# The MLP of a hybrid Mamba-2/S5 block as one row of 112 steps, with six low parts formed by transfer

## The chip, the cores and the metric

The kernel runs on one core of a Trainium2 chip. The metric is the device time of one execution in microseconds; the kernel before is given with three runs and their median. A profile is one execution recorded by the hardware profiler. PE is TensorE, DVE VectorE, ACT ScalarE, POOL GpSimd, SP SyncE.

## The reference

One decoder block over 512 tokens of width 1024, with 16 meta tokens ahead of them, all in float32. Two mixers (a Mamba-2 SSD and an S5) run side by side on one input projection and feed one output projection; then comes an MLP with a squared ReLU, and a last norm:

```python
        mix = jnp.concatenate([y_ssd.astype(h.dtype), y_s5.astype(h.dtype)], axis=-1)
        h = h + mix @ w_out[layer]
        m = _rmsnorm(h, g_mlp[layer]) @ w_up[layer]
        h = h + jnp.square(jax.nn.relu(m)) @ w_down[layer]
    return _rmsnorm(h, g_final)[:, N_META:].astype(x.dtype)
```

`w_up` is 1024 x 4096 and `w_down` 4096 x 1024. The change concerns the MLP alone, the last 350 us of some 820.

## The kernel before

**Numbers in two parts.** TensorE multiplies a shortened float32 (`F32R`). To keep the precision, each operand is split into a high part (ACT rounds it: `A.copy(hi, src)`) and a low part (DVE subtracts: `lo = src - hi`), and each product is three matmuls: high by high, high by low, low by high. The helper is `split_into` (L992 on); `split_w` makes `whi` and `wlo` of a weight block of 128x1024 numbers, `split_a` makes `ah` and `al` of an activation block of 128x512. Each of these four names has three buffers. Another way to a low part is used earlier in the kernel (L121, L122): ACT writes `-hi` into `lo`, and a DMA issued by POOL adds the source to it in memory. `add_to` (L990) is such an adding DMA.

**Fewer products.** The MLP's two matrix products are done blockwise with Strassen's scheme in the form of Winograd: 7 block products for 8, for which sums of weight blocks and of activation blocks are formed first. The hidden width is done in four quarters, each in two groups g = 0 and 1 of 512 columns.

- *Up stage* of a quarter: 14 steps, seven products (P1 to P7) for each group. A step is 24 matmuls of 256 columns with a block of `w_up` as weights and one of the token operands `opA`, `opB`, `opC` (differences of the normed tokens, `TOK`). The weights of P5, P6 and P3 are sums in a buffer of the tile `quad`: s1 = block 10 + block 11 (DVE, `vadd`), s2 = s1 + block 00 (DVE), and block 01 added by DMA for P3. P7's is block 10 plus block 00 by DMA. The products end in the tile `r`, with the squared ReLU on ACT, and additions by DVE after P2, P7 and P3.
- *Down stage* of a quarter: 14 steps, seven products for each group, named by their activations: 11, S1, S2, 12, S3, S4, 22 (`PRODUCTS`). A step is 12 matmuls of 512 columns. S1 to S4 are differences of blocks of `r` made by DVE; the weights are blocks of `w_down` or their sums T1 (DVE), T2, T3 and T4 (DMA). After a product's second group DVE adds its two banks in PSUM to the running hidden state `h_tok` (L876).

**What sets the order.** The program is written quarter by quarter: `up_blocks`, then `block_product`. Weight loads, sums and splits stand in regions of high priority (`AHEAD`), and a scheduler decides where they go on each engine; loads start as soon as a buffer is free (`quad` has six, `raw` three). Each engine executes its instructions in its own order, and an instruction that waits holds up all behind it on that engine. SP issues the loads, POOL the adding DMAs, each in order.

**Start of the MLP.** The tokens' tiles 0 and 1 give `opA`. Tiles 2 and 3 (`late`) are normed into `xs`, transposed by PE into `pt` (`turned`, L939), and combined into `opB` and `opC`. In the first quarter P1 and P2 of group 0 and P1 of group 1, which need `opA` alone, come first.

Of the kernel before, what the change touches and what calls it, by code (L numbers as in the profile page):

```python
# [53 lines left out]
def hybrid_block_kernel(ctx, tc, x, meta_tokens, g_mix, w_in, conv_w, conv_b, dt_bias, a_log, d_ssd,  # L54
# [8 lines left out]
    def dump(name, ap):  # L63
        if name in dbg:
# [6 lines left out]
    ps = ctx.enter_context(tc.tile_pool(name="ps", bufs=8, space=PSUM))  # L71
# [4 lines left out]
            "pq2": "q", "pdt": "q", "pa": "q", "par": "q", "u0": "mm"}  # L76
# [861 lines left out]
    def turned(t, k):  # L938
        pt = bank("pt")  # L939
# [41 lines left out]

    def sub(out, a, b):
        V.tensor_tensor(out=out, in0=a, in1=b, op=ALU.subtract)  # L983
# [8 lines left out]
    def split_into(hi, lo, src, by_dma=False):  # L992
        A.copy(hi, src)  # L993
        sub(lo, src, hi.bitcast(F32))
# [7 lines left out]
    def split_a(src):  # L1002
        hi = ml.tile(list(src.shape), F32R, tag="ah", name="ah", bufs=3)
        lo = ml.tile(list(src.shape), F32R, tag="al", name="al", bufs=3)
        split_into(hi, lo, src)
        return hi, lo

    def quad():
        return ml.tile([P, 2, 512], F32, tag="quad", name="quad", bufs=6)

    def up_room(raw=False):
        t = wp.tile([P, KD, P], F32, tag="raw", name="raw", bufs=3) if raw else quad()
        return t.rearrange("p a b -> p (a b)").rearrange("p (k c) -> p k c", k=4)


    t2 = up_room()
    opB = slot("opB", [P, 2, 2, 4, HT], F32R)
    opC = ml.tile([P, 3, 2, 4, HT], F32R, tag="opC", name="opC", bufs=1)
    for t in late:
        c = slice((t - 2) * P, (t - 1) * P)  # L1020
        for k in range(2):
            src = turned(t, k)
            if k == 0:
                sub(H[:, 0, 0, :, c], src, H[:, 0, 0, :, c])
                t1 = H[:, 0, 0, :, c]
            else:
                sub(t2[:, :, c], src, t1)
            A.copy(H[:, k, 1, :, c], src)
        for o, src in ((0, t2[:, :, c]), (1, t1)):
            split_into(opB[:, o, 0, :, c], opB[:, o, 1, :, c], src)  # L1030
    h12, h21, h22 = H[:, 0, 1], H[:, 1, 0], H[:, 1, 1]
    sub(h12, h12, h22)
    split_into(opC[:, 0, 0], opC[:, 0, 1], h12)
    A.mul(opC[:, 1, 0], h22, -1.0)
    neg_sub(opC[:, 1, 1], h22, opC[:, 1, 0].bitcast(F32))
    sub(t2, h21, t2)
    split_into(opC[:, 2, 0], opC[:, 2, 1], t2)
    TOK = {"P1": opA[:, 0], "P2": opA[:, 1], "P6": opB[:, 0], "P5": opB[:, 1], "P7": opC[:, 0], "P3": opC[:, 1],
           "P4": opC[:, 2]}

    class Cols:
# [7 lines left out]
        def load(self, i, k, room):  # L1049
            c0 = (8 * self.q + 4 * self.g + 2 * i) * P  # L1050
            dma(out=room, in_=w_up[0, 512 * k:512 * k + 512, c0:c0 + 2 * P].rearrange("(k p) c -> p k c", p=P))
            self.b[i, k] = room

        def sums(self):
            b = self.b
            if "S1" not in b:
                self.load(1, 0, up_room())
                self.load(1, 1, up_room(True))
                if (0, 1) not in b:
                    self.load(0, 1, up_room(True))  # L1060
                b["S1"] = up_room()
                vadd(b["S1"], b[1, 0], b[1, 1])
                b["S2"] = up_room()
                vadd(b["S2"], b["S1"], b[0, 0])
                add_to(b[1, 0], b[0, 0])

        def get(self, m):
            b = self.b
            if m == "P1":
                self.load(0, 0, up_room(not (self.q == 0 and self.g == 1)))  # L1070
                return b[0, 0]
            if m == "P2":
                if (0, 1) not in b:
                    self.load(0, 1, up_room(True))
                return b[0, 1]
            self.sums()
            if m == "P3":
                add_to(b["S2"], b[0, 1])
            return b[{"P5": "S1", "P6": "S2", "P7": (1, 0), "P3": "S2", "P4": (1, 1)}[m]]

    UP_BANK = {"P1": "X", "P2": "Y", "P5": "Z", "P6": "X", "P7": "X", "P3": "Z", "P4": "X"}
    UP_ORDER = [(g, m) for g in range(2) for m in ("P1", "P5", "P6", "P2", "P7", "P3", "P4")]

    UP_FIRST = [(0, "P1"), (0, "P2"), (1, "P1")] + [(0, m) for m in ("P6", "P5", "P7", "P3", "P4")] + UP_ORDER[8:]

    def up_blocks(q, rs):
        cs = [Cols(q, g) for g in range(2)]
        banks = {}
        for g, m in UP_FIRST if q == 0 else UP_ORDER:
            with tc.high_priority(offset=AHEAD):  # L1090
                w = split_w(cs[g].get(m))
            bk = g, UP_BANK[m]
            first = bk not in banks
            if first:
                banks[bk] = bank(f"u{g}")
            pb = banks[bk].rearrange("p (m t) -> p m t", m=2)
            x = TOK[m]
            n = 0
            for mm in range(2):
                for k in range(4):  # L1100
                    for a, b in ((0, 0), (0, 1), (1, 0)):

                        T.matmul(pb[:, mm], lhsT=w[a][:, k, mm * P:(mm + 1) * P], rhs=x[:, b, k],  # L1103
                                 start=(first and n == 0), stop=(n in (11, 23)), skip_group_check=not (first and mm == 0))
                        n += 1
            r = {(i, t): rs[g][:, i, :, t * HT:(t + 1) * HT] for i in range(2) for t in range(2)}
            if m == "P1":
                A.copy(r[0, 0], pb)
            elif m == "P2":
                sub(r[0, 0], pb, r[0, 0])  # L1110
                relu2(r[0, 0], r[0, 0])
            elif m == "P5":
                A.copy(r[1, 1], pb)
            elif m == "P6":
                A.copy(r[0, 1], pb)
            elif m == "P7":
                vadd(r[1, 1], pb, r[1, 1])
                relu2(r[1, 1], r[1, 1])
            elif m == "P3":
                vadd(r[0, 1], pb, r[0, 1])  # L1120
                relu2(r[0, 1], r[0, 1], -1.0)
            else:
                relu2(r[1, 0], pb)
# [5 lines left out]
    class Rows:  # L1129
# [8 lines left out]
        def load(self, k, n, t):  # L1138
            r0 = (8 * self.q + 4 * self.g) * P
            dma(out=t, in_=w_down[0, r0:r0 + 4 * P, 512 * n:512 * n + 512].rearrange("(j k p) c -> k p j c", k=2, p=P)[k])  # L1140
            self.b[k, n] = t

    def down_blocks(rows):

        t1 = [None, None]
        t1[0], b12a = quad(), quad()
        t1[1], b11b = quad(), quad()
        b11a, b12b = quad(), quad()
        for g, r in enumerate(rows):
            r.load(0, 0, (b11a, b11b)[g])  # L1150
        for g, r in enumerate(rows):
            r.load(0, 1, (b12a, b12b)[g])
            r.load(1, 1, spare_quads[2 + g])
            vadd(t1[g], r.b[0, 0], r.b[0, 1])
            r.b["T1"] = t1[g]
            add_to(r.b[0, 1], r.b[1, 1])
        for g, r in enumerate(rows):
            r.load(1, 0, spare_quads[g])

    def weights_of(r, m):  # L1160
        b = r.b
        if m == "T2":
            add_to(b[0, 0], b[0, 1])
        elif m == "T4":
            add_to(b[0, 0], b[1, 0])
        return b[{"11": (0, 0), "T1": "T1", "T2": (0, 0), "21": (1, 0), "T3": (0, 1), "22": (1, 1), "T4": (0, 0)}[m]]
# [31 lines left out]
    quads = slot("quads", [P, 4, 2, 512])  # L1198
    spare_quads = [quads[:, i] for i in range(4)]

    def block_product(q, rs, done):
        rows = [Rows(q, g) for g in range(2)]
        sums = [Sums(rs[g]) for g in range(2)]
        banks = {}
        with tc.high_priority(offset=AHEAD):
            down_blocks(rows)
        for n, (am, bm, bk) in enumerate(PRODUCTS):
            with tc.high_priority(offset=AHEAD):
                bs = [split_w(weights_of(rows[g], bm)) for g in range(2)]
            as_ = [split_a(sums[g].get(am)) for g in range(2)]  # L1210
            first = bk not in banks
            if first:
                banks[bk] = [bank("acct" if bk == "Y" else "acc") for _ in range(2)]
            order = [(g, s) for g in range(2) for s in range(2)]
            if n == 6:
                order.sort(key=lambda x: x[1])
            if n == 6 and q == 3:
# [112 lines left out]
```

## Time and profile before

| | us |
|---|---|
| three runs | 822.14, 826.29, 823.89; median 823.89 |
| the profiled execution | 820.66 |
| its span in the trace | 819.0 |
| PE busy, matmuls | 773.4 (94%), 4943 |
| DVE busy | 622.6 (76%) |
| ACT busy | 497.9 (61%) |
| POOL busy | 83.3 (10%) |
| MLP, up stage of quarter 0 | 470.5 to 522.2 |
| its down stage | to 561.6 |
| quarters 1, 2 and 3 | to 643.7, 726.8 and the end |

The span is the time from the first to the last recorded instruction. A row of a group of instructions has line, engine, operation, out<-in with the number of them, then the busy time, the mean of one in ns, and the idle time of its engine just before them with what ended it. In the view of waits a row has the waiting engine and line, what it waited for, the sum in us, how often, and the longest. In the timeline a row has start and length in us; in brackets stands how long the engine was idle before and who released it. In the chain of waits a row has start, length and what the time was spent on. A matmul's length holds its way through the array, so matmuls that follow each other closely overlap; their pace is the distance of their starts.

### The profile page before, as it was taken

The page shows a single profiled execution, that of the slowest core. Times are in us where ns is not written, and L with a number is a line of the kernel's source. Part 1 is how long each engine was busy: PE and PEld are TensorE (multiplying, and loading weights), DVE is VectorE, ACT ScalarE, POOL GpSimd, SP SyncE. Part 2 cuts the span into 40 slices and gives each one's busy share as a digit, 9 for nine tenths or more (in the row PEclk, how much of TensorE's full clock was granted, in tenths as well). Part 3 has the DMA queues.
Part 4 walks back from the last instruction along what each step waited for, and adds up shares of the span by engine and source line. Part 5 has one row for each costly group of instructions (what it writes and reads, how often), then busy time and mean ns, then how long its engine had stood idle before and what let it go on. Part 6 is the DMA issues. An engine that isn't in the chain of part 4 may idle for free.

```text
span 819.0 us, 13036 instructions
## 1 busy us (share of the span) xinstructions
PE 773.4 (94%) x4943; PEld 681.4 (83%) x4943; DVE 622.6 (76%) x1002; ACT 497.9 (61%) x806; POOL 83.3 (10%) x133
## 2 busy tenths in 40 slices
PE   6999999899999999999999979899989998999996
PEld 6999898898787778778888879778987898789985
DVE  4489898988785679779435486797769875987797
ACT  7578789988554753546124466654665465546665
POOL 3211000011000110010100010110111011101101
PEclk9999999999999999999999999999999999999998
DMA  8998666767664756356324058873867486747622
GB/s 242 196 226 198 140 162 143 167 146 176 151 152 132 165 133 131 101 126 231 103 99 159 1 138 273 179 181 105 226 157 168 117 216 157 167 123 186 130 51 104
DMA packets 130790, 126.10 MB, mean 154 GB/s; under 512 B 21964, under 2 KB 105848, under 8 KB 130728
## 3 DMA queue, kind: packets, MB, share of 16 engines
q1 hardware_dynamic: 121224, 90.66, 38.7%
q0 software_dynamic: 9504, 34.61, 23.2%
q8 instruction: 39, 0.64, 0.3%
q14 instruction: 23, 0.19, 0.1%
HBM read 83.76 MB, written 6.88 MB: 111 GB/s over the span
## 4 chain that ended last, share of the span: by engine, by line
PE 27%; DMA 15%; issue 14%; DVE 6%; ACT 5%; POOL 2%; SPq 0%; POOLq 0%; ACTq 0%; DVEq 0%
PE acc L832 8%; DMA quad<-raw 6%; PE pv L138 3%; PE pg L138 3%; DMA ab<-aD 3%; PE acc L1233 3%; PE acct L832 3%; DMA quad<-in_w_down_dram 2%; PE u L1103 2%; DVE wlo L983 2%; DMA raw<-in_w_up_dram 2%; ACT whi L993 2%; DVE quad L98 2%; POOL quad L990 1%; PE pyd L776 1%
## 5 line engine op out<-in xcount | busy, mean ns | idle before, releaser
L993 ACT CAST whi<-quad 128x1024 fp32r<-128x1024 f32 x73 | 76.2, 1047 | 68.1 <-PE acc L1233 28.7
L983 DVE TENSOR_TENSOR wlo<-quad,whi 128x1024 fp32r<-128x1024 f32 x73 | 89.0, 1222 | 27.3 <-ACT whi L993 27.3
L1103 PE MATMUL u<-opC,whi 128*128 128x256 f32 x384 | 71.2, 287 | 9.3 <-DVE r L98 4.8
L1233 PE MATMUL acc<-whi,al 128*128 128x512 f32 x184 | 72.5, 394 | 2.6 <-DVE al L983 2.6
L1233 PE MATMUL acc<-wlo,ah 128*128 128x512 f32 x184 | 70.9, 390 | 0.0
L1103 PEld LDWEIGHTS u<-opC,whi 128*128 128x128 f32 x384 | 59.3, 191 | 12.3 <-ACT whi L993 4.2
L1233 PE MATMUL acc<-whi,ah 128*128 128x512 f32 x184 | 65.5, 389 | 0.0
L116 ACT CAST whi<-raw 128x1024 fp32r<-128x1024 f32 x31 | 32.3, 1043 | 50.1 <-PE acc L832 31.5
L117 DVE TENSOR_TENSOR wlo<-raw,whi 128x1024 fp32r<-128x1024 f32 x31 | 38.2, 1232 | 29.6 <-ACT whi L116 29.2
L138 PE MATMUL pxb<-xhi,whi 128*128 128x264 f32 x192 | 55.5, 289 | 1.6 <-ACT xcr L694 1.6
L138 PE MATMUL pxb<-xhi,wlo 128*128 128x264 f32 x192 | 56.1, 292 | 0.0
L138 PE MATMUL pxb<-xlo,whi 128*128 128x264 f32 x192 | 55.8, 291 | 0.0
L1103 PE MATMUL u<-opC,wlo 128*128 128x256 f32 x192 | 53.1, 283 | 0.2 <-DVE wlo L983 0.2
L1103 PE MATMUL u<-opB,whi 128*128 128x256 f32 x256 | 48.2, 287 | 3.1 <-ACT whi L993 3.1
L1103 PE MATMUL u<-opA,whi 128*128 128x256 f32 x256 | 46.4, 280 | 0.0
L1233 PEld LDWEIGHTS acc<-whi,al 128*128 128x128 f32 x184 | 34.6, 188 | 12.0 <-DVE al L983 5.2
L1103 PEld LDWEIGHTS u<-opB,whi 128*128 128x128 f32 x256 | 40.9, 194 | 3.5 <-ACT whi L993 3.3
L121 POOL DMA_DIRECT2D wlo<-raw x26 | 22.3, 856 | 180.2 <-ACT xcr L694 63.4
L1233 PEld LDWEIGHTS acc<-whi,ah 128*128 128x128 f32 x184 | 34.6, 188 | 7.1
L1233 PEld LDWEIGHTS acc<-wlo,ah 128*128 128x128 f32 x184 | 34.6, 188 | 6.8
L1103 PEld LDWEIGHTS u<-opA,whi 128*128 128x128 f32 x256 | 39.5, 188 | 0.3
L122 ACT CAST whi<-raw 128x1024 fp32r<-128x1024 f32 x26 | 27.1, 1043 | 18.7 <-PE pz L138 7.3
(428 smaller groups left out, 2355.3 us busy)
## 6 DMA issues: line engine op xcount, KB each, us to landing
raw<-in_w_in_dram SPq DMA_DIRECT2D x28, 512.0 KB, 4.1
wlo<-raw POOLq DMA_DIRECT2D x26, 512.0 KB, 5.1
raw<-in_w_up_dram SPq DMA_DIRECT2D x23, 512.0 KB, 3.8
raw<-in_w_glu_dram SPq DMA_DIRECT2D x16, 512.0 KB, 4.1
raw<-in_w_out_dram SPq DMA_DIRECT2D x16, 512.0 KB, 3.5
quad<-in_w_down_dram SPq DMA_DIRECT2D x16, 512.0 KB, 5.7
quads<-in_w_down_dram SPq DMA_DIRECT2D x16, 512.0 KB, 4.6
quad<-quads POOLq DMA_DIRECT2D x16, 512.0 KB, 5.3
```

The lines of the kernel that those rows point to most:

```text
L98: V.tensor_tensor(out=out, in0=in0, in1=in1, op=ALU.add)
L116: A.copy(hi, raw)
L117: V.tensor_tensor(out=lo, in0=raw, in1=hi.bitcast(F32), op=ALU.subtract)
L121: G.dma_start(out=lo.bitcast(F32), in_=raw, accum_op=ALU.add)
L122: A.copy(hi, raw)
L138: T.matmul(ps_out, lhsT=w[a][:, k, 0:m], rhs=x[b][:, k, tok], start=(n == 0), stop=(n == len(steps) - 1))
L776: T.matmul(pyd[64 * q:64 * q + 64, o], lhsT=xdt[:, hd], rhs=Gm[h][:, hd % 8])
L832: T.matmul(acc[t], lhsT=lhs[2 * sl + k][a][:, t * P:(t + 1) * P], rhs=wt[b][:, k], start=(sl == 0 and k == 0 and n == 0), stop=(sl == n_sl ...
L983: V.tensor_tensor(out=out, in0=a, in1=b, op=ALU.subtract)
L993: A.copy(hi, src)
L1103: T.matmul(pb[:, mm], lhsT=w[a][:, k, mm * P:(mm + 1) * P], rhs=x[:, b, k], start=(first and n == 0), stop=(n in (11, 23)), skip_group_che ...
L1233: T.matmul(banks[bk][s], lhsT=as_[g][x][:, j, s * P:(s + 1) * P], rhs=bs[g][y][:, j], start=(first and g == 0 and j == 0 and i == 0), stop ...
```

## The change

The MLP is written as one row of 112 steps, 28 for a quarter (14 up, 14 down), numbered from 0. For each step a table (`at`) lists the loads and sums that are issued ahead of it; the split of step i + 2 is issued ahead of step i. Outside of the six places before step 0 no high priority is used. So in this numbering quarter 1 has its up steps at 28 to 41 and its down steps at 42 to 55: 42 and 43 are product 11 of groups 0 and 1, 44 and 45 are S1, 46 and 47 S2, 48 and 49 product 12, then S3, S4, and 54 and 55 product 22.

- Three of the seven activation blocks of each group and quarter (11, 12 and 22, blocks of `r` themselves) get `al` by transfer: ACT's multiplication by -1, then POOL's adding DMA of 128x2x256 numbers. These are 24 in all; DVE subtracts the other 32.
- Product 12 keeps its two banks in PSUM (`ybank`) over all four quarters and is added to `h_tok` once, in the last quarter: six additions fewer.
- PSUM has a pool of its own for the MLP: six banks in turn and the two that stay.
- Buffers: `quad` two instead of six, and a new tile `bquad` with four.
- In the first quarter P5 comes ahead of P6 and the steps of group 1 are mixed among those of group 0, and `opC` is made ahead of step 4.

The core of the diff:

```diff
     def split_into(hi, lo, src, by_dma=False):
-        A.copy(hi, src)
-        sub(lo, src, hi.bitcast(F32))
+        if by_dma:
+
+            A.mul(lo, src, -1.0)
+            add_to(lo.bitcast(F32), src)
+            A.copy(hi, src)
+        else:
+            A.copy(hi, src)
+            sub(lo, src, hi.bitcast(F32))
...
+    class Quarter:
...
+            for g, c in enumerate(self.cols):
+                u = 7 * g
+                self.add(u - 6, c.load(0, 0, raw_room))
+                self.add(u - 4, c.load(1, 0, lambda: as_up(quad())))
+                self.add(u - 2, c.load(1, 1, raw_room))
+                self.add(u - 1, c.s1, c.load(0, 1, raw_room))
+                self.add(u, c.s2)
+                self.add(u + 1, c.s4)
+            for g, c in enumerate(self.rows):
+                d = 14 + g
+                self.add(d - 8, c.load(0, 0, bquad))
+                self.add(d - 6, c.load(0, 1, bquad))
+                self.add(d - 5, c.load(1, 1, lambda g=g: spare_quads[2 + g]))
+                self.add(d - 3, c.load(1, 0, lambda g=g: spare_quads[g]))
+                self.add(d - 3, c.t1)
+                self.add(d - 1, c.t2)
+                self.add(d + 3, c.t4)
...
+        def split(self, i):
+            if i < 14:
+                g, m = self.ups[i]
+                self.w[i] = split_w(self.cols[g].get(m))
+            else:
...
+                n, g = divmod(i - 14, 2)
+                am, bm, _ = PRODUCTS[n]
+                self.w[i] = split_w(self.rows[g].get(bm))
+                self.a[i] = split_a(self.sums[g].get(am), am[0] != "S")
...
+        def done(self, n, s):
+            if n == 3 and self.q < 3:
+                return
...
+    for i in range(112):
+        if i == 4:
+            rest_of_tokens()
+            quads = slot("quads", [P, 4, 2, 512])
+            spare_quads = [quads[:, j] for j in range(4)]
+        ahead(i)
+        split(i + 2)
...
+        quarters[i // 28].run(i % 28)
```

`c.s1` adds blocks 10 and 11 on DVE into a `quad` and issues the DMA that makes P7's weights; `c.s2` adds block 00 on DVE, `c.s4` block 01 by DMA. `t1` adds on DVE and issues the DMA for T3; `t2` and `t4` are DMAs.

The scheduler still moves instructions of this row. The orders below show what stands where. On PE, at the start of the MLP: before, ahead of the first tokens' difference, there are the last product of the output projection (`acct`), two matmuls of the first up steps (`u_4873` is P1 of group 0, `u_4905` P2) and the transposes of tile 2.

```order
L832 MATMUL acct<-sparel,yhi 128x512
L1103 MATMUL u_4873<-opA,whi 128x256
L1103 MATMUL u_4905<-opA,whi 128x256
L941 MATMUL pt<-ident,xs 128x128 x8
L1103 MATMUL u_4873<-opA,whi 128x256
L1103 MATMUL u_4873<-opA,wlo 128x256
```

And the same place of the changed kernel:

```order
L833 MATMUL acct<-sparel,yhi 128x512
L942 MATMUL pt<-ident,xs 128x128 x16
L1220 MATMUL u<-opA,whi 128x256 x2
L1220 MATMUL u<-opA,wlo 128x256
L1220 MATMUL u<-opA,whi 128x256 x2
```

The transposes of tile 3, which stood behind two whole steps, now stand ahead of the first one.

On DVE, in the first steps of the down stage of quarter 1, before (`S_6183` and `S_6189` are S1 of groups 0 and 1; `quad<-quad,raw` is s1 of the next quarter; `al<-r` is the low part of product 11):

```order
L983 TENSOR_TENSOR al<-r,ah 128x512
L983 TENSOR_TENSOR al<-S_6183,ah 128x512
L983 TENSOR_TENSOR wlo<-quad,whi 128x1024
L983 TENSOR_TENSOR S_6189<-r 128x512
L983 TENSOR_TENSOR S_6323<-r 128x512
L986 SCALAR_TENSOR_TENSOR S_6239<-S_6189,r 128x512
L983 TENSOR_TENSOR wlo<-quad,whi 128x1024
L876 TENSOR_TENSOR h_tok<-h_tok,acc 128x512
L983 TENSOR_TENSOR al<-S_6189,ah 128x512
L876 TENSOR_TENSOR h_tok<-h_tok,acc 128x512
L98 TENSOR_TENSOR quad<-quad,raw 128x1024
L983 TENSOR_TENSOR wlo<-quad,whi 128x1024
```

And after (`S_6159` is S1 of group 0, for step 44; `S_6183` S1 of group 1, for step 45; `wlo<-bquad` is T2 of group 0, for step 46):

```order
L993 TENSOR_TENSOR al<-S_6159,ah 128x512
L993 TENSOR_TENSOR wlo<-quad,whi 128x1024 x2
L993 TENSOR_TENSOR S_6183<-r 128x512
L993 TENSOR_TENSOR S_6301<-r 128x512
L996 SCALAR_TENSOR_TENSOR S_6232<-S_6183,r 128x512
L99 TENSOR_TENSOR quad<-quad,raw 128x1024
L993 TENSOR_TENSOR wlo<-bquad,whi 128x1024
L877 TENSOR_TENSOR h_tok<-h_tok,acc 128x512
L993 TENSOR_TENSOR al<-S_6183,ah 128x512
L993 TENSOR_TENSOR al<-S_6207,ah 128x512
L877 TENSOR_TENSOR h_tok<-h_tok,acc 128x512
```

The low part of product 11 is gone from DVE, and s1 of the next quarter now stands ahead of the low part of S1 of group 1, with the split of T2 and an addition to `h_tok` between them.

On POOL, through the same down stage, before (`quad<-quad` is T2):

```order
L990 DMA quad<-quads 128x1024
L990 DMA quad<-quad 128x1024 x2
L990 DMA quad<-raw 128x1024
L990 DMA quad<-quads 128x1024 x2
L990 DMA quad<-raw 128x1024 x2
```

And after (`bquad<-bquad` is T2, `quad<-raw` the addition of s1, `bquad<-quads` T4 of both groups; the first `al` is that of step 43, the four behind are those of steps 48, 49, 54 and 55):

```order
L1000 DMA bquad<-bquad 128x1024 x2
L1000 DMA al<-r 128x2x256
L1000 DMA quad<-raw 128x1024
L1000 DMA bquad<-quads 128x1024 x2
L1000 DMA al<-r 128x2x256 x4
L1000 DMA quad<-raw 128x1024 x2
```

The additions keep their sequence, and the low parts stand among them: one behind T2, four behind T4.

More of the change, by code (lines that the diff above doesn't have):

```diff
@@ L1000, in split_w, with split_a, as_up, raw_room @@
         return hi, lo
-    def split_a(src):
+    def split_a(src, by_dma):
         hi = ml.tile(list(src.shape), F32R, tag="ah", name="ah", bufs=3)
         lo = ml.tile(list(src.shape), F32R, tag="al", name="al", bufs=3)
-        split_into(hi, lo, src)
+        split_into(hi, lo, src, by_dma)
         return hi, lo
+    def as_up(t):
+        return t.rearrange("p a b -> p (a b)").rearrange("p (k c) -> p k c", k=4)
+    def raw_room():
+        return as_up(wp.tile([P, KD, P], F32, tag="raw", name="raw", bufs=3))
     def quad():
[L1009 to L1039, printed above, removed]
+        return ml.tile([P, 2, 512], F32, tag="quad", name="quad", bufs=2)
+    def bquad():
+        return ml.tile([P, 2, 512], F32, tag="bquad", name="bquad", bufs=4)
     class Cols:
@@ L1081, in hybrid_block_kernel @@
-    UP_BANK = {"P1": "X", "P2": "Y", "P5": "Z", "P6": "X", "P7": "X", "P3": "Z", "P4": "X"}
[L1082 to L1123, printed above, removed]
@@ new lines, in f, with s1, s2 @@
+            def f():
+                c0 = (8 * self.q + 4 * self.g + 2 * i) * P
+                self.b[i, k] = t = room()
+                dma(out=t, in_=w_up[0, 512 * k:512 * k + 512, c0:c0 + 2 * P].rearrange("(k p) c -> p k c", p=P))
+            return f
+        def s1(self):
+            b = self.b
+            b["S"] = as_up(quad())
+            vadd(b["S"], b[1, 0], b[1, 1])
+            add_to(b[1, 0], b[0, 0])
+        def s2(self):
+            vadd(self.b["S"], self.b["S"], self.b[0, 0])
@@ L1291, in norm_half_second, with ahead, split, rest_of_tokens @@
                                op1=ALU.mult)
-    for q in range(4):
-        rs = [ml.tile([P, 2, 2, SEQ], F32, tag="r", name="r") for _ in range(2)]
-        up_blocks(q, rs)
-        if q == 3:
+    quarters = [Quarter(q) for q in range(4)]
+    def ahead(i):
+        for qu in quarters:
+            qu.ahead(i - 28 * qu.q)
+    def split(i):
+        if i < 112:
+            quarters[i // 28].split(i % 28)
+    with tc.high_priority(offset=AHEAD):
+        for i in range(-6, 0):
+            ahead(i)
+        split(0)
+        split(1)
+    t2 = as_up(bquad())
+    opB = slot("opB", [P, 2, 2, 4, HT], F32R)
+    opC = ml.tile([P, 3, 2, 4, HT], F32R, tag="opC", name="opC", bufs=1)
+    TOK = {"P1": opA[:, 0], "P2": opA[:, 1], "P6": opB[:, 0], "P5": opB[:, 1], "P7": opC[:, 0], "P3": opC[:, 1],
+           "P4": opC[:, 2]}
+    for t in late:
+        c = slice((t - 2) * P, (t - 1) * P)
+        for k in range(2):
+            src = turned(t, k)
+            if k == 0:
+                t1 = H[:, 0, 0, :, c]
+                sub(t1, src, t1)
+                split_into(opB[:, 1, 0, :, c], opB[:, 1, 1, :, c], t1)
+            else:
+                sub(t2[:, :, c], src, t1)
+                split_into(opB[:, 0, 0, :, c], opB[:, 0, 1, :, c], t2[:, :, c])
+            A.copy(H[:, k, 1, :, c], src)
+    h12, h21, h22 = H[:, 0, 1], H[:, 1, 0], H[:, 1, 1]
+    def rest_of_tokens():
+        sub(h12, h12, h22)
+        split_into(opC[:, 0, 0], opC[:, 0, 1], h12)
+        A.mul(opC[:, 1, 0], h22, -1.0)
+        neg_sub(opC[:, 1, 1], h22, opC[:, 1, 0].bitcast(F32))
+        sub(t2, h21, t2)
+        split_into(opC[:, 2, 0], opC[:, 2, 1], t2)
+    for i in range(112):
[3 more added lines that the diff above has]
+            spare_quads = [quads[:, j] for j in range(4)]
+        ahead(i)
+        split(i + 2)
+        if i == 98:
             os = slot("os", [P, 4, DM])
             sqj = ml.tile([P, SEQ], F32, tag="rl", name="sqj", bufs=1)
-        block_product(q, rs, finish if q == 3 else lambda n, t, ch: None)
+        quarters[i // 28].run(i % 28)
 _INS = ['x', 'meta_tokens', 'g_mix', 'w_in', 'conv_w', 'conv_b', 'dt_bias', 'a_log', 'd_ssd', 'g_ssd', 'lam_re',
```

232 lines of the change are left out of this document (139 added, 93 removed).

## The prediction

> **What bounds the kernel now.** The first part of the page asks which engine is full.
>
> ```profile
> PE 773.4 (94%) x4943; PEld 681.4 (83%) x4943; DVE 622.6 (76%) x1002; ACT 497.9 (61%) x806; POOL 83.3 (10%) x133
> ```
>
> PE is, and the change leaves its 4943 matmuls as they are, so time can only come out of PE's idle stretches and its clock. Up to the MLP the two programs are alike; the MLP starts at 470.5 us. The table by stages (the up stage of quarter 0, its down stage, then quarters 1, 2 and 3) shows where PE stands still there.
>
> ```profile
> core 0: us, PE busy (x) PEld busy (x) DVE busy (x) ACT busy (x) POOL busy (x), PEclk, DMA share, GB/s
> 470.50:522.20 51.70, 43.25 (x334) 41.30 (x332) 38.37 (x43) 31.15 (x45) 4.98 (x7) 0.97 0.74 204
> 522.20:561.60 39.40, 38.26 (x176) 31.06 (x177) 37.81 (x49) 24.78 (x33) 4.95 (x6) 1.00 0.70 161
> 561.60:643.70 82.10, 78.80 (x501) 70.63 (x500) 64.34 (x75) 48.20 (x64) 8.51 (x10) 1.00 0.67 167
> 643.70:726.80 83.10, 79.71 (x505) 71.52 (x504) 65.37 (x77) 48.22 (x64) 8.48 (x10) 1.00 0.66 165
> 726.80:808.00 81.20, 80.52 (x523) 73.45 (x522) 67.17 (x86) 50.73 (x74) 7.67 (x9) 1.00 0.46 104
> ```
>
> Length less PE's busy time gives its idle time: 8.45, 1.14, 3.30, 3.39 and 0.68 us, 16.96 in all. Quarter 0 also lost clock: 0.97 granted over 51.7 us is some 1.5 us. That is the whole prize, 2.2% of the span; nothing else in this change can make it faster. The view of waits, from 470 us on, says what PE stood still for.
>
> ```profile
> PE u L1103 <- ACT whi L993: 6.5, 5, 3.1
> PE u L1103 <- DVE r L98: 4.8, 3, 1.7
> PE acc L1233 <- DVE al L983: 2.6, 3, 1.0
> PE u L1103 <- DVE wlo L983: 1.3, 2, 1.1
> ```
>
> Three kinds recur in quarters 0 to 2: a split high part that is late (3.1 at the start, else about 1), the addition to r after P3 (1.7 at the most), a low part al (1.0 at the most). DVE holds most of them; in the down stage of quarter 0 it works 37.81 of 39.40 us.
>
> **What PE needs for a step.** The timeline gives the pace where nothing is late.
>
> ```profile
> 508.92 0.40 PE L1103 MATMUL u<-opA,whi 128*128 128x256 f32 x2
> ...
> 511.02 0.39 PE L1103 MATMUL u<-opA,whi 128*128 128x256 f32 x2
> 468.93 0.39 PE L832 MATMUL acct<-sparel,yhi 128*128 128x512 f32 x1
> ...
> 469.84 0.39 PE L832 MATMUL acct<-spareh,yhi 128*128 128x512 f32 x1
> ```
>
> Eighteen matmuls of 256 columns start in 2.10 us and four of 512 in 0.91: 0.117 and 0.228 each. An up step (24) takes 2.8 us, a down step (12) 2.74.
>
> **The change part by part. Work taken off DVE.**
>
> ```profile
> L983 DVE TENSOR_TENSOR al<-r,ah 128x512 fp32r<-128x512 f32 x24 | 16.5, 687 | 3.1 <-ACT ah L993 3.1
> L876 DVE TENSOR_TENSOR h_tok<-h_tok,acc 128x512 f32<-128x512 f32 x46 | 30.3, 681 | 0.2
> L993 ACT CAST ah<-r 128x512 fp32r<-128x512 f32 x24 | 14.8, 616 | 0.3
> ```
>
> The 24 low parts leave DVE (16.5 us) and so do six additions to h_tok (4.1), 20.6 in all. ACT gets 24 multiplications of the size of ah, 14.8 us; it is idle for a third of every stage, so I cost them at nothing, except where one stands ahead of a split (below). POOL gets 24 DMAs. By itself none of this moves PE: what counts is which operand is last at each step, so I followed each operand of after's order with these durations.
>
> **Up stages of quarters 1 to 3: two waits go.** In quarter 1 of before the chain and DVE's timeline show their causes.
>
> ```profile
> 588.92 7.08 DMA quad<-raw
> 601.29 1.23 DVE L98 TENSOR_TENSOR quad<-quad 128x1024 f32<-128x1024 f32 x1 [2.88 <-DMA quad<-in_w_down_dram]
> ```
>
> The addition by transfer for P7 ran into its neighbour in the queue, took 7.08 us, and P7's whi was late (0.87 us for PE). Later DVE stood 2.88 us at the sum T1 for a load, and the addition to r after P3 was queued behind it (1.5). In after's row T1 stands three steps, 8.4 us, behind its nearest load, and P7's addition five steps ahead of P7. I take both waits as gone; what is late next has a slack of 0.9 us at the least. That is 2.4 us of idle gained in quarters 1 and 2 each, 0.45 in quarter 3.
>
> **Down stages: the next quarter's sum in front of the low parts.** DVE's rows of the order show `quad<-quad,raw` (s1 of the next quarter) ahead of a split, an h_tok addition and `al<-S_6183`, for which step 45 waits. Let the down stage begin at 0. PE executes 39 matmuls before it needs this al: 39 x 0.228 = 8.9. ACT and DVE have first the relu and square of P4, then the splits.
>
> ```profile
> 607.51 0.54 ACT r L1126
> 609.88 0.97 ACT whi L993
> 610.87 1.24 DVE wlo L983
> 617.19 1.23 DVE L98 TENSOR_TENSOR quad<-quad,raw 128x1024 f32<-128x1024 f32 x1 [0.34 <-DVE h_tok L876]
> 618.33 1.22 DVE L983 TENSOR_TENSOR wlo<-quad,whi 128x1024 fp32r<-128x1024 f32 x1
> 619.47 0.69 DVE L983 TENSOR_TENSOR al<-S,ah 128x512 fp32r<-128x512 f32 x1
> 620.07 0.69 DVE L983 TENSOR_TENSOR S<-r 128x512 f32<-128x512 f32 x1
> ```
>
> These follow each other 1.14 us apart for 1024 columns and 0.60 for 512. So 0.25 + 2 x 0.54 + 0.97 + 1.14 = 3.45 is when wlo of step 44 ends; its quad then takes a load for s1, issued at 3.5. How long a load takes to land is the first unknown.
>
> ```profile
> DMA to landing us min/median/max: 3.6/4.7/9.3
> ```
>
> That is tile raw in the MLP; the loads of w_up into quad have a median of 3.6 there. I take 4.1, between the two: s1 starts at 7.6, where DVE would be free at 6.8. Then 1.14 for s1, 1.14 for wlo, 0.60 and 0.60: al is there at 11.1, PE stands 2.2 us. The bounds: 1.4 with a load that is on time, 7.4 with one that takes 9.3. In before this sum stood behind the low parts, and al cost 0.8.
>
> **Low parts by transfer.** They share POOL's queue with the additions, the second unknown: before has no transfer of 256 KB that adds.
>
> ```profile
> 567.33 4.54 DMA quad<-raw
> q0 software_dynamic: 432, 1.57, 61.7%
> out_dram<-os SPq DMA_DIRECT2D x2, 512.0 KB, 2.7
> out_dram<-os SPq DMA_DIRECT2D x4, 256.0 KB, 2.5
> ```
>
> An addition of 512 KB that is alone lands 4.5 us after its issue. Between 618 and 632 us three of them were queued: 1.57 MB in 61.7% of 14 us, 2.9 us each. Half the size should move in 1.45 us and land alone after 4.5 - 1.45 = 3.1 (an estimate from these two rows); it is not worse than 4.5, the whole size, if its shorter pieces cost no more than twice as much a byte. The plain stores of 512 and 256 KB differ by only 0.2. I take 1.45 in the queue. The first low part of a quarter that matters, step 43, waits on POOL behind the addition of T2 and lands near 5.8, needed at 5.9: 0.2 us lost. That of step 48 stands behind s1's addition (issued at 8.7, first bytes 1.5 later) and both T4: 10.2 + 3 x 2.9 + 1.45 = 20.3. PE comes there after six steps and the wait above: 16.4 + 2.2 + 0.6 = 19.2, so 1.1 lost; the bounds are 0 (transfers of 2.5 us) and 2.7 (transfers of 3.4). Steps 49, 54 and 55 have over 1.3 us of slack.
>
> [...]
>
> **Start and up stage of quarter 0.** The order shows PE's sixteen transposes ahead of the first step, where eight stood and then two steps. The last eight need xs of tile 3, which hangs on the sums of the projection, not on PE's order.
>
> ```profile
> 473.67 0.75 DVE L867 SCALAR_TENSOR_TENSOR xs<-h_tok,rh,gains 128x512 f32<-128x512 f32 x1 [0.66 <-POOL rh L865]
> 483.93 0.50 PE L1103 MATMUL u<-opB,whi 128*128 128x256 f32 x2 [3.08 <-ACT whi L993]
> 485.51 0.58 PE L1103 MATMUL u<-opB,wlo 128*128 128x256 f32 x1 [1.07 <-DVE wlo L983]
> 485.89 0.63 PE L1103 MATMUL u<-opB,whi 128*128 128x256 f32 x2
> 486.32 0.41 PE L1103 MATMUL u<-opB,wlo 128*128 128x256 f32 x1
> ```
>
> So xs is ready at 474.4: eight transposes end at 471.35, and PE idles 3.0 us. In before PE idled 3.08 and 1.07 at 481 to 485, and then ran at half speed (three matmuls in 0.63 us). In after step 3 waits some 0.75 us. Step 4 waits for DVE, which from 474.4 on has eight operations of 1.14 and seven of 0.60, 13.3 us, to reach the low part of its weights' split, and waits for ACT between them: I put it at 490.4 (2.85 us of waiting). Step 8 waits 1.9 us for loads that land about 499 and the sum and split behind them. With 3.0 that is 8.5 us idle, as before's 8.45. The clock's 1.5 us is hidden if it falls between, since step 8 starts when its loads are there, at 503.3. I count 1.5 for it and 0.8 for fewer restarts (PE loses 0.16 us beyond each wait; five fewer). The bounds are 0 and 4.3.
>
> **The sum, on the profiled execution.** Idle after: 8.5 in the up stage of quarter 0; 0.2 + 1.7 + 1.1 = 3.0 in its down stage (s1 there waits less long); 0.2 + 2.2 + 1.1 = 3.5 in quarters 1 and 2 each; 0.9 in quarter 3, which has no next s1. Together 19.4 against 16.96, 2.4 more; less 2.3 for clock and restarts: no change. The execution took 820.66 us with a span of 819.0; the median of the three runs, 823.89, lies 3.2 above it, and the three reach from 822.1 to 826.3. I predict 823.5.
>
> **The rivals.** *Faster.* The loads for s1 land in 3.6 us or less and the queue of POOL drains faster than I count: 1.4 us in three down stages and no other wait, 6.5 at the start. Idle is 4.2 + 6.5 + 0.5 = 11.2, 5.8 less than before, and with the 2.3 some 8 us: 816. For it: DVE loses 20.6 us of work and the up stages have slack. Against it: the al stays behind s1 whatever the load does.
>
> *Slower.* The load for s1 lands late. It is issued among the next quarter's other loads and POOL's additions, and the view of raw shows 9.3 as its longest. Everything on DVE behind s1 then waits, and PE with it, in quarters 0, 1 and 2. Each us costs 3 us. A landing of 5.5 instead of 4.1 adds 4.2 us and decides; 7 adds 8.7: 832. For it: the median of 4.7 for raw. Against it: w_up into quad has 3.6.
>
> *The fixed row isn't fixed.* The order shows PE's steps still interleaved by the scheduler; the gains and losses above come from its places, and this is in the forecast.
>
> **How the numbers follow.** A measurement of this kernel can tell about 0.5%, 4.1 us, from no change. No change: 0.44, with its own range of 819 to 829. The faster rival: 0.27. The rule of no queue by rows: if transfers drain in 2.5 us or less and nothing else moves, 3.9 us go and 819.6 is left; 0.05, counted as faster. [...] The slower rival: 0.24. So faster 0.32, same 0.44, slower 0.24. The range goes down to 813: 816, less 2 with the start at its bound of 4.3, less 1 for the scatter of the runs. It goes up to the slower case's 832.
>
> **What will show it.** Right: no waits of PE for the P3 addition or for a whi in the up stages of quarters 1 to 3; a wait of 1.4 to 3 us for a DVE al about 9 us into each of the first three down stages, with DVE's s1 before it idle for a load; a wait near 1 us for an al of POOL some 19 us into them. Wrong: a load for s1 that lands before DVE asks for it, additions that leave the queue less than 2.5 us apart, or a step 8 that starts other than near 503.

## The result and the profile after

The changed kernel takes 871.08 us (median of 4 runs, 869.35 to 874.25); the kernel before takes 824.44 (4 runs, 822.14 to 826.29). The ratio is 1.0571, with a 95% interval of 1.053 to 1.0613: 5.7% slower, some 47 us. The profiled execution has a span of 872.5 us. The table by stages, in the same columns as before (up stage and down stage of quarter 0, then quarters 1, 2 and 3; the limits are those of the same work):

```profile
474.80:531.60 56.80, 45.91 (x335) 43.09 (x333) 37.21 (x41) 31.59 (x45) 6.93 (x8) 0.94 0.72 190
531.60:589.00 57.40, 44.53 (x175) 35.04 (x176) 34.79 (x43) 27.30 (x38) 10.23 (x10) 0.86 0.73 161
589.00:684.00 95.00, 85.94 (x507) 75.38 (x507) 61.45 (x68) 51.49 (x71) 15.77 (x16) 0.93 0.71 161
684.00:777.50 93.50, 85.02 (x504) 74.97 (x503) 61.45 (x68) 51.02 (x70) 15.72 (x16) 0.94 0.72 163
777.50:862.00 84.50, 80.02 (x519) 72.62 (x517) 63.31 (x79) 54.75 (x82) 15.96 (x17) 1.00 0.51 100
```

Together these stages take 387.2 us, before 337.5. The MLP also starts 4 us later here; the programs are alike up to that place, and the kernels below that are made from the changed one start their MLP anywhere between 470 and 478 us, so I don't count it as an effect of the transfers. What moves it wasn't tried. PE's idle time (length less busy time) is 10.89, 12.87, 9.06, 8.48 and 4.48 us, 45.8 in all, where it was 16.96: 28.8 more. The rest is clock: a stretch of length T at a granted clock of g lacks T x (1 - g) of full speed, and the five rows lack 3.4 + 8.0 + 6.7 + 5.6 + 0 = 23.7 us, where before lacked 1.5. So 28.8 us of waiting and 22 of clock, 51 by this reckoning, account for the 49.7. The view of waits says for what PE waits, and the list of DMAs how long the new transfers take:

```profile
PE acc L1261 <- DMA al<-r: 11.2, 4, 5.0
PE ybank L1261 <- DMA al<-r: 10.5, 4, 4.0
PE acc L1275 <- DMA al<-r: 9.1, 4, 2.5
PE u L1220 <- ACT whi L1009: 4.4, 7, 2.2
PE u L1220 <- DVE wlo L993: 3.6, 4, 1.6
PE pt L942 <- ACT xs L867: 2.8, 1, 2.8
PE u L1220 <- DVE r L99: 1.7, 3, 0.9
al<-r POOLq DMA_DIRECT2D x24, 256.0 KB, 6.9
```

The low parts by transfer are waited for 12 times, three in each quarter (products 11, 12 and 22): 30.8 us. All other idle time of PE comes to 15.0 us, where before had 17.0 in all. A transfer of 256 KB lands 6.9 us after its issue in the median, longer than the additions of twice its size in before (5.3 to 5.6). What such a wait does to the clock stands in PE's timeline at step 15 (product 11 of group 1 in quarter 0), and in the granted clock right behind two waits:

```profile
538.79 0.39 PE L1261 MATMUL acc<-whi,al 128*128 128x512 f32 x1
544.17 0.79 PE L1261 MATMUL acc<-whi,al 128*128 128x512 f32 x1 [4.99 <-DMA al<-r]
544.76 0.63 PE L1261 MATMUL acc<-wlo,ah 128*128 128x512 f32 x1
545.19 0.63 PE L1261 MATMUL acc<-whi,ah 128*128 128x512 f32 x1
...
736.58 0.63 PE L1261 MATMUL acc<-whi,al 128*128 128x512 f32 x1 [2.07 <-DMA al<-r]
...
544.20:547.60 3.40, 3.40 (x8) 2.73 (x9) 0.89 (x2) 0.00 (x0) 0.00 (x0) 0.50 0.01 5
736.60:740.00 3.40, 3.40 (x9) 2.65 (x10) 1.09 (x1) 0.00 (x0) 0.00 (x0) 0.53 0.22 74
```

After the wait the matmuls follow each other at 0.43 us in place of 0.23; 8 or 9 of them fit in 3.4 us instead of 15. A wait of two microseconds can thus cost about 1.7 more. It needn't: behind the two of the twelve waits that were 1.35 and 2.48 us long (both in quarter 3) the clock is full (1.00 over 3.4 us).

### The profile page after: what moved, and what is told of

Its sections match the earlier page's. It is cut to its first block, busy times and chain, and to the rows that moved or that the text cites. A ratio compares the mean times of both kernels' runs of the same rounds, so it can differ in the third digit from the quotient of the medians.

```text
span 872.5 us, 13110 instructions
## 1 busy us (share of the span) xinstructions
PE 796.6 (91%) x4943; PEld 697.2 (80%) x4943; DVE 607.3 (70%) x972; ACT 510.4 (58%) x830; POOL 110.3 (13%) x157
## 4 chain that ended last, share of the span: by engine, by line
PE 30%; DMA 21%; issue 7%; DVE 6%; ACT 5%; POOL 1%; SPq 0%; ACTq 0%; POOLq 0%; DVEq 0%
PE acc L833 8%; DMA al<-r 7%; PE acc L1261 6%; DMA quad<-raw 5%; DMA ab<-aD 3%; DMA quad<-in_w_up_dram 3%; PE ybank L1261 3%; PE pg L139 3%; DVE wlo L993 3%; PE acct L833 3%; PE pv L139 2%; PE acc L1275 2%; ACT whi L1009 2%; DVE quad L99 1%; PE pyd L777 1%
## 5 line engine op out<-in xcount | busy, mean ns | idle before, releaser
L993 DVE TENSOR_TENSOR wlo<-quad,whi 128x1024 fp32r<-128x1024 f32 x40 | 49.0, 1225 | 53.4 <-ACT whi L1009 50.8
L1261 PE MATMUL acc<-whi,al 128*128 128x512 f32 x160 | 65.1, 407 | 12.0 <-DMA al<-r 11.2
L1009 ACT CAST whi<-quad 128x1024 fp32r<-128x1024 f32 x40 | 41.8, 1045 | 53.4 <-PE acc L1275 15.9
L1009 ACT CAST whi<-bquad 128x1024 fp32r<-128x1024 f32 x34 | 35.5, 1045 | 53.0 <-PE acc L1261 30.3
L1261 PE MATMUL acc<-wlo,ah 128*128 128x512 f32 x160 | 63.7, 405 | 0.0
L117 ACT CAST whi<-raw 128x1024 fp32r<-128x1024 f32 x31 | 32.4, 1044 | 52.5 <-PE acc L833 31.6
L1261 PE MATMUL acc<-whi,ah 128*128 128x512 f32 x160 | 59.6, 407 | 1.8 <-DVE h_tok L877 1.1
L993 DVE TENSOR_TENSOR wlo<-bquad,whi 128x1024 fp32r<-128x1024 f32 x34 | 41.5, 1222 | 25.3 <-ACT whi L1009 25.2
L1261 PEld LDWEIGHTS acc<-whi,al 128*128 128x128 f32 x160 | 31.2, 195 | 21.0 <-DMA al<-r 12.9
L1000 POOL DMA_DIRECT2D al<-r x24 | 29.6, 1233 | 102.9 <-ACT al L1005 100.3
```

The source lines that it names most:

```text
L117: A.copy(hi, raw)
L1000: G.dma_start(out=t, in_=src, accum_op=ALU.add)
L1261: T.matmul(banks[s], lhsT=at[x][:, j, s * P:(s + 1) * P], rhs=wt[y][:, j], start=(fresh and g == 0 and j == 0 and k == 0), stop=(g == 1 an ...
```

## The experiments

Two theories at first. **L**: the transfers are late and everything follows from that. **O**: the order of the row is at fault (sums ahead of low parts, two `quad` buffers, splits only two steps ahead), and the transfers are merely where it shows. A third, **C**: 24 more transfers slow down the loads and additions of others, whenever they are issued. All times below are medians beside runs of the kernel before on the same chip.

**No transfer.** In the changed kernel:

```diff
-                self.a[i] = split_a(self.sums[g].get(am), am[0] != "S")
+                self.a[i] = split_a(self.sums[g].get(am), False)
```

> The changed kernel with all low parts subtracted on DVE again; row of steps, buffers, banks kept. Theory L (late transfers): the 30.9 us that PE waits for an al by DMA and the some 19 us of half clock behind these waits go, so the time is within 4 us of before: 820 to 828. Theory O (the order): the fixed row, with two quad buffers and splits two steps ahead, is what is late, and the transfers are only where it shows: the time stays above 850 us.

Measured: 824.83 us against 822.01, ratio 1.0023 (0.9998 to 1.0048). The loss is gone within what these runs can tell (2.8 us are left, the interval reaches from 0 to 4), 44 of the 47 us; O falls. The stages of this kernel show what the rest of the change does:

```profile
470.40:527.30 56.90, 45.51 (x336) 43.04 (x334) 37.88 (x42) 31.12 (x45) 5.70 (x7) 0.94 0.68 185
527.30:572.00 44.70, 42.99 (x197) 36.18 (x198) 39.93 (x50) 25.98 (x34) 4.24 (x5) 0.96 0.71 177
572.00:652.50 80.50, 79.09 (x504) 71.33 (x504) 64.38 (x75) 48.39 (x64) 8.48 (x10) 1.00 0.70 170
652.50:731.50 79.00, 78.74 (x505) 71.39 (x504) 64.43 (x75) 48.41 (x64) 8.48 (x10) 1.00 0.71 174
731.50:808.50 77.00, 75.98 (x503) 69.63 (x501) 64.14 (x83) 49.94 (x73) 7.67 (x9) 1.00 0.42 90
```

Idle 11.39, 1.71, 1.41, 0.26 and 1.02 us: quarters 1 and 2 save 5 us of waiting against before (3.30 and 3.39 there), and quarter 0 gives it back in waits and clock (0.94 and 0.96).

**The transfers alone.** In the kernel before, `split_into` got the branch of the change and the loop of the down stage uses it:

```diff
-            as_ = [split_a(sums[g].get(am)) for g in range(2)]
+            as_ = [split_a(sums[g].get(am), am[0] != "S") for g in range(2)]
```

> The kernel before with the same 24 low parts (products 11, 12 and 22) by transfer and nothing else. L: the transfers land 6 to 8 us after their issue here too and three buffers of al leave them at most two steps, 5.5 us: 845 to 875 us, with PE waiting 20 us or more for al by DMA. O: within 8 us of before, below 832.

Measured: 860.79 us, ratio 1.0458 (1.041 to 1.0507). Its waits:

```profile
PE acc L1238 <- DMA al<-r: 11.1, 5, 3.6
PE acct L1238 <- DMA al<-r: 9.7, 4, 3.5
PE acc L1229 <- DMA al<-r: 2.1, 1, 2.1
```

22.9 us in another order of the same work. L holds; the transfers bring 39 us by themselves.

**Only product 22.** In the changed kernel, `am == "22"` in place of `am[0] != "S"`.

> The changed kernel with only product 22 by transfer (8 of 24). L: its own four waits of some 2.3 us remain, 9 us, with some 1.6 us of half clock behind each, 15 us above the kernel without transfers: 833 to 843. O: above 850. If the shares don't add up (within 3 us of the kernel without transfers, or above 850), the waits hang on each other.

Measured: 840.7 us, ratio 1.0217 (1.0187 to 1.0246): 15.9 above the kernel without transfers, for 8 transfers of 24. The size came out, its parts didn't:

```profile
PE acc L1275 <- DMA al<-r: 13.3, 4, 4.0
```

The four waits are 13.3 us, not 9. The transfers start no later ahead of their use than in the changed kernel (3.7 to 4.2 us, there 4.2), but in quarters 0 to 2 they landed 8.2, 6.9 and 7.3 us after their issue, where that kernel's took 6.5, 6.3 and 6.3. Why wasn't tried.

**The transfers started earlier.** The multiplication and the adding DMA go out four steps ahead of their step, into two buffers of their own. To make room, `al` has two buffers and the scratch of the last squares stands in a `raw`.

```diff
+    def low_ahead(src):
+        lo = ml.tile(list(src.shape), F32R, tag="at", name="at", bufs=2)
+        A.mul(lo, src, -1.0)
+        add_to(lo.bitcast(F32), src)
+        return lo
...
+        if i + 4 < 112:
+            quarters[(i + 4) // 28].early((i + 4) % 28)
         split(i + 2)
```

> The changed kernel with each low part by transfer begun four steps ahead of its step in two buffers of its own (al has two for DVE's, the scratch of the last squares stands in raw). L: the waits of products 12 and 22 go (some 20 of 31 us and two thirds of the lost clock), that of product 11 stays, since its r is only then ready: 832 to 845 us. C (the added transfers slow down the loads and additions of others, whenever they are issued): above 855. O: above 850.

Measured: 823.89 us, ratio 1.0013 (0.9994 to 1.0033). This is better than L expected: product 11 isn't waited for either, since the scheduler puts its transfer ahead of the additions of T2 in POOL's queue (issued at 607.77 in quarter 1, T2 at 614.65). No row of a transfer is left among PE's waits, and yet the view of the tile says

```profile
DMA to landing us min/median/max: 3.7/4.6/8.0
```

The longest, those of product 22 in quarters 0 to 2, take 7.3 to 8.0 us, no less than in the changed kernel (6.3 to 7.7); they only start earlier. Those of product 12 and the second of product 11 also land sooner, after 3.8 to 5.0 us in place of 6.8 to 8.5 in these quarters, since they now stand ahead of the additions in POOL's queue. All 24 transfers are there, so C falls too for this order.

**Own buffers, but two steps ahead.** The same with `i + 2` in place of `i + 4`.

> As the kernel whose transfers start four steps ahead, but issued only two steps ahead in the program, as in the change; what stays is that the low parts by transfer have two buffers of their own, so that a transfer needn't wait until step i - 3 has released al. If the shared three buffers hold the transfers back: PE's waits for them stay under 8 us in all, 824 to 834 us. If the place in the program does: 850 or more.

Measured: 838.38 us against 823.63, ratio 1.0188 (1.0161 to 1.0215): between the two cases.

```profile
PE acc L1278 <- DMA at<-r: 10.4, 4, 4.1
```

Only product 11 is still waited for, four times. For products 12 and 22 a buffer that is free is enough, because the scheduler then moves the multiplication up; for product 11 the place in the program decides. So of the 47 us about 32 hang on the shared buffers and 14 on the lead.

**The six additions back.** In the kernel without transfers, product 12 starts its banks anew in each quarter and is added to `h_tok` each time:

```diff
-            fresh = fresh and not (bk == "Y" and self.q > 0)
...
-            if n == 3 and self.q < 3:
-                return
```

> The changed kernel without transfers, and product 12 added to h_tok in every quarter again: six additions of 0.68 us, 4.1 us, back on DVE. They lie beside PE's work: within 2 us of the kernel without transfers (824.8). If DVE's load decides the waits for al and for the P3 addition: 3 to 6 us slower.

Measured: 823.43 us against 823.63, ratio 1.0009 (0.9989 to 1.0029). The additions lie beside PE's work.

**Sixteen transfers.** With the early start, but product 11 on DVE: `if am in ("12", "22")`.

> Products 12 and 22 by transfer four steps ahead in own buffers, product 11 on DVE. L: no wait of PE for a transfer, 821 to 827 us. If every transfer costs something wherever it stands (C): 825 to 835, above the kernel without transfers.

Measured: 835.6 us against 823.63, ratio 1.0139 (1.011 to 1.0169). The time is at the top of C's range, but not by its cause: PE waits for no transfer, and for DVE instead. First the wait, then DVE's timeline in quarter 0.

```profile
PE acc L1278 <- DVE al L993: 11.6, 4, 3.9
...
543.72 1.23 DVE L99 TENSOR_TENSOR quad<-quad,raw 128x1024 f32<-128x1024 f32 x1 [0.34 <-DMA quad<-in_w_up_dram]
544.86 1.29 DVE L993 TENSOR_TENSOR al<-S,ah 128x512 fp32r<-128x512 f32 x2
```

The sum s1 of the next quarter stands right ahead of the low part, having waited for its load. In quarter 1 s1 starts at 627.43 after DVE has idled 1.79 us, and the low part at 629.18; PE waits 3.89. Two `al` buffers serve product 11 as well here, but DVE goes from s1 to the low part without idling, so at this place no buffer held it back; whether the two buffers led the scheduler to this order wasn't tried.

**Sixteen transfers in the kernel before.** Begun two products ahead, in own buffers:

```diff
+            if n in (1, 4):
+                later = [low_ahead(sums[g].get("12" if n == 1 else "22")) for g in range(2)]
-            as_ = [split_a(sums[g].get(am)) for g in range(2)]
+            as_ = [split_a(sums[g].get(am), later[g] if am in ("12", "22") else None) for g in range(2)]
```

> The kernel before with products 12 and 22 by transfer, begun two products ahead in two buffers of their own (al has two): the order of before, 16 subtractions (11 us) fewer on DVE. If DVE's work is what makes al and the P3 addition late: 816 to 820. If these waits come from loads and queues instead: within 2 us of before, 820 to 824. If the transfers are late: above 828.

Measured: 842.33 us against 823.63, ratio 1.0234 (1.0206 to 1.0262). None of the three: no transfer is late, DVE has 11 us less to do, and the kernel is slower.

```profile
PE acc L1244 <- DVE al L983: 12.6, 4, 4.2
PE u L1112 <- ACT whi L993: 11.6, 5, 3.1
...
590.38 1.20 POOL L990 DMA_DIRECT2D at<-r  x1 [8.82 <-ACT at L1013]
591.09 1.40 POOL L990 DMA_DIRECT2D quad<-quads  x1
592.59 0.85 POOL L990 DMA_DIRECT2D quad<-raw  x1
```

On DVE s1 stands right ahead of that low part, as in the kernel above, after 1.36 us of idling in quarter 0 and 1.71 in quarter 1; in before it stands behind. The second row is 5 us more than in before: in the up stages of quarters 1 to 3 PE waits 2.3 to 2.7 us for P7's high part, where before had 0.9 at the most. The rows of POOL show why: a low part and an addition go out right ahead of P7's addition, which lands 8.3 us after its issue, before 7.1. So here C has a share of the loss, which wasn't measured by itself. Less work on an engine that isn't the bound buys nothing when its order gets worse.

**s1 behind the low part.** T1 of group 1 is made ahead of that of group 0, so that the load for s1 gets the `quad` that is freed a step later: `self.add(12 - g, c.t1)`. Once with the early transfers, once without transfers.

> The kernel with transfers four steps ahead in own buffers, and in it the sums T1 of the two groups in the other sequence, so that the load for the next quarter's s1 gets the quad that is freed a step later: s1 then stands behind the low part of step 45 on DVE in all three quarters. The prediction's step on s1: the waits for that low part (2.6, 0.9 and 0.5 us, with 1.5 us of slow clock behind the first) go, 4 to 6 us: 818 to 820. If something else holds that low part back (ah, or the two buffers of al): within 1.5 us of 823.9.

> The same exchange in the kernel without transfers, where the wait for the low part of step 45 was 1.7 and 0.5 us, too short for a slow clock: 1 to 3 us less than its 824.8, so 822 to 824. If something else holds it back: no change, 824 to 826.

Measured: 829.07 us against 821.99, ratio 1.0101 (1.0078 to 1.0125), and 827.45, ratio 1.0066 (1.004 to 1.0093). Both slower, against what I expected. DVE's timeline in quarter 1 of the first, and PE's wait behind it:

```profile
625.24 1.23 DVE L99 TENSOR_TENSOR quad<-quad,raw 128x1024 f32<-128x1024 f32 x1 [1.88 <-issue]
626.38 1.22 DVE L993 TENSOR_TENSOR wlo<-bquad,whi 128x1024 fp32r<-128x1024 f32 x1
627.52 0.69 DVE L993 TENSOR_TENSOR S<-r 128x512 f32<-128x512 f32 x1
628.12 0.69 DVE L993 TENSOR_TENSOR al<-S,ah 128x512 fp32r<-128x512 f32 x1
...
628.86 0.50 PE L1278 MATMUL acc<-whi,al 128*128 128x512 f32 x1 [2.47 <-DVE al L993]
```

Only in quarter 0 had s1 stood ahead of the first low part of S1's second group; there the exchange took away that wait of 2.57 us, and one of 2.68 for an `ah` of ACT came in its place. In quarters 1 and 2 s1 stood between the low parts of steps 45 and 46 and still does, but it starts later: in quarter 1 6.6 us behind the issue of its load, where it was 5.0. DVE idles 1.88 us in front of it (the profile doesn't name what for; the load is likely), and PE waits 2.47 us for the low part of step 46 (2.17 in quarter 2), where 0.86 and 0.52 were. Behind the wait of quarter 2 the clock falls (0.66 over 3.4 us), behind that of quarter 1 it doesn't (the matmuls start 0.24 us apart). The waits moved and grew.

**Loads of quarter 0 held back.** The four loads into `quads` wait for a result of step 5, by a tiny copy on ACT into their buffer.

> The kernel with transfers four steps ahead in own buffers; the four loads of w_down that the down stage of quarter 0 needs last (into quads) wait for a result of step 5 (four tiny copies on ACT make them wait). In that kernel they are issued at 489 to 491 us, and the w_up load behind them takes 12.4 us, P7's addition 8.8: PE waits 1.9 and 0.8 us with some 1.6 us of slow clock. If these loads are what makes both late, the three go: 819 to 821, below before. If the loads only move the crowd to T1 and T3: 823 to 827.

> The same in the kernel without transfers, whose waits there are 1.4 and 0.8 us with 1.6 us of slow clock: 821 to 823, level with before. If the loads only move the crowd: 824 to 828.

Measured: 827.42 us against 823.1, ratio 1.0039 (1.0018 to 1.0061), and 824.21, ratio 1.0017 (0.9998 to 1.0036). The aim was met: P7's addition takes 5.1 us in place of 8.8. But the crowd moved to the second addition behind it, which took 8.9, where it was 5.7:

```profile
PE u L1239 <- DVE wlo L993: 5.3, 2, 4.8
```

No kernel here is faster than the one before.

## Why the prediction was wrong

- **What bounds the kernel.** Right. What the five stages lost is PE's idle time and PE's clock.
- **Work taken off DVE is worth nothing by itself.** Right: six additions back (4.1 us) and 24 subtractions back (16.5 us, the kernel without transfers beside the one with early transfers) cost nothing; 16 fewer of them in the kernel before didn't help.
- **Two waits of the up stages go.** Right where the transfers are out of the way: without them, idle time in quarters 1 and 2 falls from 6.7 to 1.7 us, and of the P3 additions one of 0.77 is left in quarters 1 to 3.
- **s1 ahead of the low part.** The mechanism is in the traces (the changed kernel with sixteen early transfers shows it in two rows). The size was right in quarter 0 of the kernel without transfers, 1.7 us as predicted, and too large behind it, 0.5 and 0 for 2.2 each: with the subtractions back on DVE, s1 stands a step further back there. In the changed kernel itself PE waits 0.7 us for such a low part in quarter 0 and not at all behind it; the waits for transfers come first. Of the rivals, a late s1 is what the exchange of the two T1 brought about in quarters 1 and 2.
- **Start and up stage of quarter 0.** Idle 8.5 was predicted, the kernel without transfers has 11.4, and the 2.3 us for clock and restarts were not gained: the row of its stage has a clock of 0.94.
- **Low parts by transfer: this step failed.** I had 0.2 us lost at step 43, 1.1 at step 48, and "Steps 49, 54 and 55 have over 1.3 us of slack": some 4.5 us in all (1.3 in each of quarters 0 to 2 and most of the 0.9 of quarter 3). It was 30.8: in quarter 1 2.80 at step 43, 3.00 at step 48 and 2.14 at step 54. Most of the 22 us of clock came with it. Without the transfers the kernel's idle time is 15.8 us, by the table of its stages, and 19.4 less 4.5, 14.9, had been predicted. That these are so close is luck in part: the up stage of quarter 0 has 2.9 us more than predicted, and quarters 1 and 2 together 2.7 less. And that kernel lacks 5.2 us of clock in quarter 0, where before lacked 1.5 and I had counted on a gain. So the transfers make some 44 us of the error, and the clock of quarter 0 the rest. Three things were wrong in this term.

*When a transfer starts.* I counted from the time when its block of `r` is there and POOL's queue is free. ACT's and POOL's timelines ahead of step 26 (product 22 of group 0 in quarter 0; its like in quarter 1 is 54) show on what it starts, and PE's what it waits:

```profile
577.39 1.05 ACT L1009 CAST whi<-bquad 128x1024 fp32r<-128x1024 f32 x1 [1.15 <-PE acc L1261]
578.35 0.63 ACT L1005 ACTIVATE al<-r 128x512 fp32r<-128x512 f32 x1
...
579.28 1.18 POOL L1000 DMA_DIRECT2D al<-r  x1 [19.09 <-ACT al L1005]
...
585.78 0.50 PE L1275 MATMUL acc<-whi,al 128*128 128x512 f32 x1 [2.31 <-DMA al<-r]
```

The multiplication stands on ACT behind the split of the weights, and that waited for PE to release one of three `whi`. Its `al` comes from three buffers too. Each is released when PE is done with the step three before, so a transfer begins two steps, 5.5 us, ahead of its use at the best, and after the split and the multiplication are done there are 4.2 left. POOL had been idle for 19 us. I had said that ACT's multiplications cost nothing, "except where one stands ahead of a split"; it was standing behind one that mattered. That the start is the cause and not the speed is shown for products 22 and 12 by the two kernels with buffers of their own: in the one with a lead of two steps those of product 22 take 6.4 to 8.2 us in quarters 0 to 2, those of product 12 up to 7.2, and PE waits for none of them. For product 11 the start and the landing changed together; with its issue at 607.77 and the down stage beginning at 616.31 in quarter 1 of the kernel with early transfers, its lead would have covered the slowest landing, 8.5, as well.

*How long a transfer takes.* Alone it lands in 3.7 us, inside my bounds of 3.1 to 4.5. For products 11 and 12 the neighbours in POOL's own queue were worse than I had counted, and for product 22 I had left out the loads of SP. First POOL's timeline ahead of step 15 and the queues of DMA in the 3.1 us after the issue of its like in quarter 1 (634.9 to 638.0); then the queues in the 3.8 us after the transfer of product 22 above was issued, and in the 3.7 us after the first one of quarter 3:

```profile
535.95 0.84 POOL L1000 DMA_DIRECT2D bquad<-bquad  x1 [2.04 <-DVE wlo L993]
536.49 1.52 POOL L1000 DMA_DIRECT2D al<-r  x1
...
q0 software_dynamic: 171, 0.63, 105.9%
...
q1 hardware_dynamic: 329, 0.64, 71.3%
...
q0 software_dynamic: 272, 0.26, 48.6%
q1 hardware_dynamic: 215, 0.20, 15.7%
```

In the first stretch POOL's queue (q0) alone fills the engines, with the additions of T2 that stand ahead (the share adds up the time of all packets and can pass 100%); behind the issue for step 48 it is the same, 107.0% from 652.4 to 655.0. In quarter 1 the low part of step 43 lands 8.8 us into the down stage, where I had put 5.8; PE came for it at 6.1, where I had put 5.9. In the second, loads (q1) take the engines and q0 doesn't appear at all: the transfer lands after 6.5 us. In the third it lands after 3.7, with 48.6% of 3.7 = 1.8 us of data, where I took 1.45. Why the loads go first wasn't tried.

*What a wait costs.* I priced each wait at its length and 0.16 us, as much as a matmul of 512 columns lasts (0.39) beyond its pace (0.228), though the trace of before had a stretch at half speed behind two waits (a clock of 0.51 from 485.5 to 488.9). The five stages lacked 22 us of clock more than before.

The faster rival had 1.4 us of waiting in each of three down stages and none for a transfer. The kernel with early transfers comes near that (2.6, 0.9 and 0.5), the change doesn't, and its start took 10.9 us in place of that rival's 6.5. The case with 0.05, in which no low part is late and 3.9 us go, didn't come about either: PE waited for twelve of the 24 transfers. The slower rival was the wrong mechanism, and its 832 was far too little. The range ended 39 us below the result.

## What to carry to other kernels

Moving work to an engine with time to spare is a change of latency before it is a change of load: ask how early the new path can start, from the release of its buffers and the row in which it is issued, and put its slowest landing against that lead, not its median when alone. Then price a wait of PE at its length plus up to 1.7 us more for the clock: behind nine of the twelve waits for transfers here it was 0.50 to 0.72 over 3.4 us, behind the other three 1.00. And after every edit read the order again: with a scheduler, taking work away from an engine can put what is left in a worse place.

## What the runs showed of the hardware that I had not expected

The clock can fall after short waits. Behind PE's wait of 1.7 us in the up stage of quarter 0 of before, and one of 1.53 in quarter 1, the clock is full; behind 1.80 in the kernel without transfers (the wait ends at 527.3) it is 0.56. The wait in that kernel's view of waits, and the windows of 3.4 us behind the three, before first:

```profile
PE u L1220 <- DVE r L99: 2.6, 2, 1.8
...
522.20:525.60 3.40, 3.40 (x26) 3.35 (x27) 2.83 (x3) 3.33 (x5) 1.56 (x2) 1.00 0.71 134
605.00:608.40 3.40, 3.40 (x26) 3.31 (x27) 2.68 (x3) 3.34 (x6) 0.84 (x1) 1.00 0.99 159
527.30:530.70 3.40, 3.40 (x17) 3.40 (x18) 3.40 (x4) 3.13 (x5) 0.84 (x1) 0.56 0.92 173
```

Behind another wait of the kernel without transfers, the 1.7 us for `al` in the down stage of quarter 0, the clock is 1.00 from 541.9 to 545.3. Ten of the twelve waits for transfers in the changed kernel are of 2 us and more; behind nine of them the clock is 0.50 to 0.72 over 3.4 us, but not behind all: behind the one of 2.48 us, and behind the 2.8 us for xs at the start of the changed kernel's MLP, it is 1.00. The length alone doesn't decide: all eleven kernels here with the fixed row have this wait, of 2.76 or 2.77 us, at the same place, and over the 3.4 us behind it the clock is 1.00 in five of them and 0.59 to 0.70 in the other six. What else decides wasn't tried. The lowest clock in such a stretch is 0.50, and behind the wait of 2.07 us the slow pace of 0.43 us lasts from 736.58 to 740.00, 3.4 us; waits as short as 1.80 and 2.07 us were followed by one here.

The other surprise is the transfer itself: 256 KB in pieces of 1 KB took 1.8 us in the queue, where 512 KB in additions of before took 2.9, so that halving the bytes saved little more than a third.
